# A decoder block on one core: the branch weights moved behind z's steps with a third place, one combine moved behind them, and half of z's first tokens reloaded as rows

## The chip, the cores and the metric

The kernel runs on one core of a Trainium2 chip. A core has five engines that work side by side, each on its own queue of instructions: TensorE (PE, matrix products; its weight loads are listed apart as PEld), VectorE (DVE), ScalarE (ACT), GpSimd (POOL) and SyncE (SP, which here only issues transfers). Transfers are carried by sixteen DMA engines and may be issued by SP, POOL and ACT. An engine starts an instruction only when the instruction ahead of it on its own queue is under way and the semaphores that it names are up, so an instruction that waits also holds all that stands behind it on that engine. The metric is the device time of one launch in microseconds (us).

## The reference

The reference is one layer of a decoder on 2,048 tokens of width 1,024, all in 32-bit floats. Cut to what matters:

```python
h = rmsnorm(x, norm_pre_mix)
proj = h @ w_in                       # q k v | u z | gate_a gate_b
y_attn = dilated_attention(rope(q), rope(k), v)          # three groups, softmax over the groups
z = layernorm(gelu(proj_z))                              # 512 channels
sz = w_spatial (lower triangle, per 128 tokens) @ z + b_spatial
y_gmlp = gelu(proj_u) * sz
merged = sigmoid(gate_a) * (y_attn @ w_branch_attn) + sigmoid(gate_b) * (y_gmlp @ w_branch_gmlp)
x = x + rmsnorm(merged @ w_out, norm_post_mix)
x = x + rmsnorm(relu(rmsnorm(x) @ w_mlp_in) ** 2 @ w_mlp_out, norm_post_mlp)
```

`y_attn` combines three groups of heads: per token and head the three partial outputs are scaled by a softmax over three log-denominators and added. The kernel calls that step the combine.

## The kernel before

The tokens are worked in four chunks of 512 (0 to 3), and chunks in two halves (0 and 1 are half 0). Every 32-bit operand of a large product is kept as two parts, a high part (`hi`, the value rounded to the matmul's type) and a low part (`lo`, value minus `hi`), and `mm3` (L94) makes one product of three matmuls: hi·hi, hi·lo and lo·hi (L95, L96, L97). `split` (L67) makes the two parts from a raw value: a copy that rounds (L70 on ACT, L72 on POOL) and a subtraction (L78, on DVE or POOL).

Most of the program is written as generators that PE steps through: `steps(n)` advances the matmul stream (`fill`) by n steps of three matmuls, and the code between two calls places work of the other engines there. On PE the order of the instructions is the written one. On the other engines a scheduler may move an instruction, but what stands in `with behind():` is issued only after the instruction of each of these engines that stands ahead of it in the program.

The stretch that this document is about is the end of the input products, before the branches are merged:

- `gates()` (L666) makes the gate and u columns. In its last phase (half 0) it also issues from a list `ins`, one entry a step (two at two of the steps), the loads of the next stage: `hT_b0`, the normalised tokens of chunk 0 transposed (both parts, eight loads of 512 KB from `hb_d`, where the parts were stored), and `w_z0`, the z weights (eight loads of 512 KB from `wz_d`). Raw tokens lie in `hT_d` too. An entry of the list `todo` is split between, by ACT and POOL. The tiles `ga0` to `ga11` hold gate and u columns on their way out.
- z of half 0: `z_00` to `z_03` (chunk 0) and `z_10` to `z_13` (chunk 1), each eight steps over the eight blocks k of the width. Steps are counted by `n` in the loop at L1091. On the way it loads `hT_b1` (raw rows, four loads) and splits them (ACT and POOL, at n 12, 15, 18, 21), loads and splits the six branch weights `wb0` to `wb5` (`load_wb`, `split_wb`: POOL issues the load and rounds, DVE subtracts), and works the last chunk's combine. A branch weight's raw rows `wbraw` (512 KB) lie in one of two places; a load into a place waits for the DVE subtraction of the weight that lay there.
- the combine of chunk 1 (L964) reads its partial outputs from `cw`. DVE makes maximum `M`, differences `E`, then ACT the exponential, DVE the sums `Z`, the reciprocal and the scaled `E`; ACT and DVE scale the outputs (L990, L993), DVE adds them (L995, L996), PE transposes the result (`yt_10`, `yt_11`, L1001), ACT copies it and stores it to `yad`.
- the merge of chunk 2 begins behind z: `load_y` brings six operands `yt`, all split by POOL (twelve operations); `b` are the products with the branch weights, `gates` the gate columns, multiplied in by DVE (L1189); `sz` is the spatial product of `z`; `woraw` are raw rows of the output weights.

Two waits on SP belong to the picture. Eight semaphores are used in turn for the transfers that SP and ACT issue, and a transfer waits until the earlier one on its semaphore has landed. So `early_gates` (L1144) waits for the two stores `yad` of the last combine.

Of the kernel before, what the change touches and what calls it, by code (L numbers as in the profile page):

```python
# [8 lines left out]
F32 = mybir.dt.float32  # L9
# [7 lines left out]
P = 128  # L17
S = 2048
D = 1024
# [8 lines left out]
def f32(ap):  # L28
    return ap.bitcast(F32) if ap.dtype != F32 else ap
# [12 lines left out]
def block_kernel(ctx, tc, a, out):  # L42
    nc = tc.nc
    pe, act, dve, pool, sp = nc.tensor, nc.scalar, nc.vector, nc.gpsimd, nc.sync
    x = a["x"]

    def stack(es, name, bufs=1, side=None, space=None):
        kw = dict(name=name, bufs=bufs, reuse_waits="tile")
        if side:
            kw["side"] = side  # L50
        if space is not None:
            kw["space"] = space
        return es.enter_context(tc.tile_pool(**kw))
# [13 lines left out]
    def split(hi, lo, src, hi_eng="act", lo_eng="dve"):  # L67

        if hi_eng == "act":
            act.activation(hi, src, AF.Copy)  # L70
        elif hi_eng == "pool":
            pool.tensor_scalar(hi, src, 1.0, 1.0, op0=OP.mult, op1=OP.mult)  # L72
        else:
            dve.tensor_copy(hi, src)
        if behind_product is not None and lo_eng == "dve":
            behind_product.append((lo, src, f32(hi)))
        else:
            (pool if lo_eng == "pool" else dve).tensor_sub(lo, src, f32(hi))  # L78
# [70 lines left out]
    hT_d = dtile([4, P, KT, 512], "hTd")  # L149
# [15 lines left out]
    e1 = ExitStack()  # L165
    hp = stack(e1, "hp", 1)
    wp = stack(e1, "wp", 2)
# [7 lines left out]
    def behind():  # L175

        es, t = ExitStack(), mybir.EngineType
        for e in (t.Activation, t.DVE, t.Pool, t.SP):
            es.enter_context(tc.issue_after(next(i for i in reversed(nc.cur_bb.bb.instructions) if i.engine == e)))
        return es  # L180

    hT = {}
# [178 lines left out]
    with ExitStack() as e1a:  # L361
# [118 lines left out]
        for half in range(2):  # L480
# [19 lines left out]
            for n, (g, which) in enumerate(qk):  # L500
                w = nxt
# [112 lines left out]
    LAST = len(seq) - PAIRS[0]  # L614
# [51 lines left out]
    def gates():  # L666

        bank, todo, out_, ins = {}, [], [], []
        slots = [None, hp.tile([P, 2, 2, 4, 512], F32R, name="opB", tag="hT", bufs=2)]
        zs = wp.tile([P, 8, 512], F32, name="gz", tag="w", bufs=3)  # L670
        zs = [zs[:, n] for n in range(8)]
        xs = [st.tile([P, 512], F32, name=f"gx{n}", tag="ev", bufs=3) for n in range(3)]
        g_["b"].update({(1, 1): hT[2][:, :, :4], (1, 2): hT[2][:, :, 4:]})
        phases = [(half, ops) for half in (1, 0) for ops in PHASES]
        starts, t = {}, 0
        for n, (half, ops) in enumerate(phases):
            starts[t] = n
            t += PAIRS[half] * len(ops)
        for t, (half, i, n) in enumerate(seq):
            if t in starts:  # L680
                ph, t0 = starts[t], t
                if ph + 1 < len(phases):
                    s = (ph + 1) % 2
                    if not slots[s]:
                        slots[s] = hp.tile([P, 2, 2, 4, 512], F32R, name="opA", tag="hT", bufs=2)
                    for j, i2 in enumerate(phases[ph + 1][1]):
                        new = operand(phases[ph + 1][0], i2, slots[s][:, j])
                        ins += new[0]
                        todo += new[1]
                else:  # L690
                    hs = reload_h(0)
                    ins += hs[:4] + ws[4:6] + hs[4:6] + ws[6:] + hs[6:]
            elif todo and (t - t0) % 3 == 1 and t > t0 + 1:
                w, k = todo.pop(0)
                with behind():
                    split(w[:, 0, k:k + 2], w[:, 1, k:k + 2], f32(w)[:, 1, k:k + 2], "act", "pool")
            if t == LAST - 4:
                ws = want(5)
                ins += ws[:4]
            if t == LAST:  # L700
                g_["ends"] = g_["vs"] + zs[8:]
            for n_ in (t + PIECES,) if t < LAST else {0: (4, 5), 1: (6, 7), 2: (8,), 3: (9,)}.get(t - LAST, ()):
                piece(n_ if t < LAST else LAST + n_)
            split_piece(t + SPLITS)
            if i in (1, 6, 5, 4):
                bank[n] = psum_mm(f"g{half}{i}{n}")
            p, w, h = bank[n], g_["w"].pop(t), g_["b"][half, i]
            for k in range(4):
                for m, (l, r) in enumerate(((0, 0), (0, 1), (1, 0))):
                    pe.matmul(p, w[:, l, k], h[:, r, k], start=i in (1, 6, 5, 4) and not k and not m,  # L710
                              stop=k == 3 and m == 2, skip_group_check=True)
                if (t, k) == (3, 2) and late:
                    sz_out(*late.pop(0))
                yield
            if t == 3:
                a = [ga.tile([P, 512], F32, name=f"ga{n_}", tag=f"ga{n_}", bufs=1) for n_ in range(12)]
                xs += a[:7]
                zs += a[7:9]
                vs = a[9:11]
                g_["vs"] = vs + xs[8:] + zs[8:]  # L720
                g_["raws"] += a[11:]
            x, z, fn = xs[n], zs[n], AF.Copy if n < 8 else AF.Gelu_apprx_tanh
            while out_:
                sp.dma_start(*out_.pop())
            for _ in range(2 if half and i == 4 or t in (LAST + 5, LAST + 7) else 1):
                if ins:
                    sp.dma_start(*ins.pop(0))
            if i == 1:
                act.activation(x, p, AF.Copy)
            elif i == 2:  # L730
                act.activation(z, p, fn)
                o = z, 0, 0
            elif i == 6:
                dve.tensor_add(z, x, p)
            elif i == 7:
                dve.tensor_add(x, x, p)
            elif i == 5:
                if (half, n) == (0, 0):
                    g_["vs"] = a[9:11]
                v = g_["vs"].pop(0)  # L740
                g_["vs"].append(v)
                dve.tensor_add(v, x, p)  # L742
                o = v, 1, 1
            elif i == 3:
                dve.tensor_add(z, z, p)
                o = z, 0, 1
            else:
                dve.tensor_add(x, x, p)  # L748
                o = x, 1, 0
            if n > 7 and i in (5, 3, 4):  # L750
                act.activation(o[0], o[0], fn)
            if i in (2, 5, 3, 4):
                c, dst = 2 * half + o[2], gate_d if n < 8 else u_d
                out_.append((dst[n % 8 * 2 + o[1], :, c * 512:(c + 1) * 512], o[0]))
        sp.dma_start(*out_.pop())
        yield
# [302 lines left out]
    def combined(*order):  # L1059
        for n, k in order:  # L1060
            steps(n)
            with behind():
                next(cs[k])

    combined((0, 0), (4, 1), (8, 0), (3, 0), (3, 0), (2, 2), (6, 1), (3, 1), (3, 1), (1, 0),
             (10, 2), (3, 2), (3, 2), (1, 1), (19, 2))
    steps(75 - 69)
    ec.close()
    ega.close()

    e2r = ExitStack()
    wbp = stack(e2r, "wbp", 1, side="right")
    wb = [wbp.tile([P, 2, D], F32R, name=f"wb{k}") for k in range(6)]
    wb_raw = {}

    def load_wb(k):
        wb_raw[k] = wp.tile([P, D], F32, name=f"wbraw{k}", tag="raw", bufs=2)
        pool.dma_start(wb_raw[k], a["w_branch"][:, k, :])

    def split_wb(k):  # L1080
        with behind():
            split(wb[k][:, 0], wb[k][:, 1], wb_raw.pop(k), "pool", "dve")
# [4 lines left out]
    next(sg)  # L1087
    while not cw:
        steps(1)
    todo = {22: (3,), 24: (3,), 27: (3,), 38: (3,)}  # L1090
    for n in range(1, 56):  # L1091
        steps(1)
        if zin:
            sp.dma_start(*zin.pop(0))
        if n in (12, 15, 18, 21):
            k, h = (n - 12) // 3 * 2, hT[1]
            with behind():
                split(h[:, 0, k:k + 2], h[:, 1, k:k + 2], f32(h)[:, 1, k:k + 2], "act", "pool")
        if n in (24, 28, 32, 36, 42, 48):
            split_wb((24, 28, 32, 36, 42, 48).index(n))  # L1100
        if n in (4, 6, 25, 29, 33, 37):
            load_wb((4, 6, 25, 29, 33, 37).index(n))
        if n == 48:
            next(sg)
        for k in todo.get(n, ()):
            combined((0, k))
# [402 lines left out]
    for n, c in enumerate(chunks):  # L1509
        if n:  # L1510
            mg = merge(c, yt, {0: flush, 2: flush}, merge_sums if c == 0 else merge_sums_last if c == 1 else None)
        for i in range(4):
# [10 lines left out]
            if n == 3 and i == 1:  # L1523
# [7 lines left out]
                for o, (q, n_) in enumerate(FIRST):  # L1531
                    raw = gtp.tile([P, 512], F32, name=f"ar{n_}_{q}", tag=f"gt{o % 2}", bufs=3 - o % 2)
# [234 lines left out]
    for n, z in enumerate(last_ones):  # L1767
# [28 lines left out]
        elif n == 9:  # L1796
# [4 lines left out]
            w = s1p.tile([P, 2, 512], F32R, name="spot0")  # L1801
# [33 lines left out]
    begun, ybank, left, todo = set(), {}, {}, {}  # L1835
# [128 lines left out]
    for k, (_, n, i) in enumerate(yorder):  # L1964
# [10 lines left out]
        if i == 1 and more:  # L1975
# [6 lines left out]
            if nth in (4, 5) and g + 1 < NQ // 2 - 1:  # L1982
                w = 2 * g + nth - 2
# [102 lines left out]
```

## Time and profile before

| what | time |
|---|---|
| three runs | 2663.45, 2666.44 and 2670.65 us, median 2666.44 |
| the profiled execution | 2663.08 us, span 2661.4 us |
| PE busy | 2619.8 us, 98% of the span |
| z of half 0, from its first matmul to the first of the merge's `b` | 1015.66 to 1077.2 us of the span |

Times in the rows below are microseconds from the start of the span. A row of the timeline has start, duration, engine, line, operation, the tile written and the tiles read, and how many alike are put together (x4); in square brackets stands how long the engine had been idle before it and what ended that. A row of waits has engine, line, operation that waited and what it waited for, then the sum of the waits, their count and the longest. In a row of the windows stand, after the stretch's length, the busy time and the number of instructions of PE, PEld, DVE, ACT and POOL, then the clock that was granted to TensorE (1 is full speed), the share of the DMA engines' time that was busy, and GB/s.

### The profile page before, as it was taken

What the parts mean: (1) busy time and instruction counts of PE and PEld (TensorE: products, weight loads), DVE (VectorE), ACT (ScalarE), POOL (GpSimd) and SP (SyncE); (2) the same over time, 40 slices, a digit from 0 to 9 for tenths busy, and PEclk for the clock granted to TensorE, in tenths of its full rate; (3) what the DMA queues carried; (4) which work ended last, traced back from release to release, by engine and by line L of the source; (5) the groups of instructions that cost most, each with busy time, mean ns of one, the idle gap of its engine ahead of it and who ended that gap; (6) DMA issues with size and microseconds to landing.
All of it is one profiled execution on the core that took longest, in us unless ns stands there. A gap on an engine that the chain in (4) does not pass through costs nothing. (4 is left out here: it accounts for less than half of the span.)

```text
span 2661.4 us, 35503 instructions
## 1 busy us (share of the span) xinstructions
PE 2619.8 (98%) x12458; PEld 2186.9 (82%) x12458; DVE 1665.8 (63%) x2793; ACT 1090.9 (41%) x2283; POOL 1207.1 (45%) x1099
## 2 busy tenths in 40 slices
PE   9999999999999998999999999999999999999998
PEld 8888888888888886788878888888888888888886
DVE  5676665535443466755676665645437888888866
ACT  5213111254455443444446555655545333323334
POOL 0363354374454554311324463233215776676645
PEclk9999999999999998999999999999999999999999
DMA  8779778888888897744556464644343222222235
GB/s 319 285 246 323 266 228 289 294 282 248 291 287 242 236 310 277 242 154 153 207 199 254 146 225 149 222 139 119 119 147 107 87 71 73 87 88 87 87 115 210
DMA packets 389285, 526.21 MB, mean 198 GB/s; under 512 B 57009, under 2 KB 242097, under 8 KB 388082
## 3 DMA queue, kind: packets, MB, share of 16 engines
q1 hardware_dynamic: 299472, 430.79, 49.5%
q0 software_dynamic: 15856, 54.80, 5.5%
q10 hardware_dynamic: 73778, 38.35, 4.8%
q8 instruction: 98, 1.61, 0.3%
q14 instruction: 81, 0.66, 0.1%
HBM read 340.67 MB, written 183.17 MB: 197 GB/s over the span
## 5 line engine op out<-in xcount | busy, mean ns | idle before, releaser
L1937 PE MATMUL ya<-T_spots,s 128*128 128x512 f32 x1176 | 289.3, 390 | 0.7 <-ACT T_spots L70 0.6
L70 ACT ACTIVATE s<-sraw 128x768 fp32r<-128x768 f32 (+1 forms) x184 | 127.2, 696 | 330.3 <-POOL sraw L1738 155.7
L1937 PEld LDWEIGHTS ya<-T_spots,s 128*128 128x128 f32 x1176 | 220.6, 188 | 47.3 <-ACT T_spots L70 0.9
L78 DVE TENSOR_TENSOR s<-sraw,s 128x512 fp32r<-128x512 f32 x172 | 184.1, 1095 | 8.5 <-ACT s L70 8.5
L1408 PE MATMUL aa<-B,A 128*128 128x512 f32 x768 | 182.4, 390 | 1.5 <-ACT xs L1422 0.9
L1379 POOL TENSOR_TENSOR s<-w1r 128x512 f32<-128x512 f32 x32 | 42.3, 1322 | 308.7 <-DVE S L78 256.1
L710 PE MATMUL g<-opA,spots 128*128 128x512 f32 x672 | 171.4, 399 | 1.9 <-DVE cv L742 1.9
L1408 PEld LDWEIGHTS aa<-B,A 128*128 128x128 f32 x768 | 143.9, 188 | 32.0 <-ACT xs L1422 1.3
L710 PE MATMUL g<-opB,spots 128*128 128x512 f32 x648 | 164.3, 398 | 0.2 <-DVE ga L748 0.2
L1937 PE MATMUL yc<-T_spots,s 128*128 128x512 f32 x624 | 159.7, 389 | 0.0
L95 PE MATMUL x<-hT_a,wq 128*128 128x512 f32 x384 | 149.8, 390 | 0.0
L97 PE MATMUL x<-hT_a,wq 128*128 128x512 f32 x384 | 149.6, 389 | 0.0
L96 PE MATMUL x<-hT_a,wq 128*128 128x512 f32 x384 | 149.6, 389 | 0.0
L710 PEld LDWEIGHTS g<-opA,spots 128*128 128x128 f32 x672 | 121.6, 189 | 23.9 <-issue 2.2
L78 POOL TENSOR_TENSOR spots<-gr,spots 128x512 fp32r<-128x512 f32 x98 | 127.5, 1304 | 22.7 <-DMA gr<-in_w_in_dram 15.7
L1937 PEld LDWEIGHTS yc<-T_spots,s 128*128 128x128 f32 x624 | 117.2, 188 | 24.3
L710 PEld LDWEIGHTS g<-opB,spots 128*128 128x128 f32 x648 | 116.9, 189 | 21.6 <-issue 0.6
L70 ACT ACTIVATE hl<-r 128x512 fp32r<-128x512 f32 x48 | 30.4, 632 | 235.4 <-POOL r L321 89.0
L960 DVE TENSOR_REDUCE o<-po 128x256 f32<-128x512 f32 x48 | 33.2, 692 | 133.6 <-PE po L959 133.5
L1737 POOL TENSOR_TENSOR sraw<-sraw 128x256 f32<-128x256 f32 x56 | 41.8, 747 | 161.8 <-DVE s L78 158.8
L72 POOL TENSOR_SCALAR spots<-gr 128x512 fp32r<-128x512 f32 x86 | 54.9, 638 | 132.1 <-PE g L710 100.7
L78 POOL TENSOR_TENSOR T_spots<-w2r,T_spots 128x512 fp32r<-128x512 f32 x70 | 104.4, 1519 | 7.3 <-ACT T_spots L70 7.3
(427 smaller groups left out, 6990.3 us busy)
## 6 DMA issues: line engine op xcount, KB each, us to landing
w1r<-in_w_mlp_in_dram SPq DMA_DIRECT2D x64, 512.0 KB, 3.8
sraw<-sd SPq DMA_DIRECT2D x128, 256.0 KB, 3.2
qk<-hl SPq DMA_DIRECT2D x24, 1024.0 KB, 5.7
qq<-qk SPq DMA_DIRECT2D x96, 256.0 KB, 5.2
w2r<-in_w_mlp_out_dram SPq DMA_DIRECT2D x16, 1024.0 KB, 7.8
sd<-u ACTq DMA_DIRECT2D x63, 256.0 KB, 3.5
g<-gated SPq DMA_DIRECT2D x58, 256.0 KB, 4.7
gr<-sgd SPq DMA_DIRECT2D x53, 256.0 KB, 4.8
```

Of the source, the lines that this page charges most:

```text
L70: act.activation(hi, src, AF.Copy)
L72: pool.tensor_scalar(hi, src, 1.0, 1.0, op0=OP.mult, op1=OP.mult)
L78: (pool if lo_eng == "pool" else dve).tensor_sub(lo, src, f32(hi))
L95: pe.matmul(ps, lh, rh, start=start, stop=False)
L96: pe.matmul(ps, lh, rl, start=False, stop=False)
L97: pe.matmul(ps, ll, rh, start=False, stop=stop)
L710: pe.matmul(p, w[:, l, k], h[:, r, k], start=i in (1, 6, 5, 4) and not k and not m, stop=k == 3 and m == 2, skip_group_check=True)
L960: dve.tensor_reduce(ot[:, :, j * 64:(j + 1) * 64], po.rearrange("p (b h e) -> p b e h", b=4, h=2), axis=AX.X, op=OP.add)
L1379: pool.tensor_add(s1, a21, a22)
L1408: pe.matmul(p, w[:, l, k, :], h[:, r, k, :], start=i in (1, 6, 5) and not k and not n, stop=k == 3 and n == 2, skip_group_check=True)
L1737: pool.tensor_add(a22, a21, a22)
L1937: pe.matmul(p, s[:, l], w[r], start=i in (1, 2, 5) and not m and not o, stop=m == 1 and o == 2, skip_group_check=True)
```

## The change

Four things are changed, all between about 970 and 1090 us of the span.

- In `gates()`, of the eight loads of `hT_b0` the first four (both parts of k 0 to 3) are replaced by two loads of raw rows from `hT_d` into the place of the low part. ACT and DVE split them (ACT rounds, DVE subtracts). The list `ins` has ten entries where it had twelve, and 1 MB less is read.
- A third place for branch weights, `wr`, laid over `ga0` and `ga1`, takes `wbraw2` and `wbraw5`. The loads now stand behind what is ahead of them, at n 8, 9, 10, 23, 25, 27 (before 4, 6, 25, 29, 33, 37), and the splits at n 23, 25, 27, 36, 38, 40 (before 24, 28, 32, 36, 42, 48).
- The combine of chunk 1 moves from n 22, 24, 27, 38 to n 43, 45, 48, 60, behind all splits of branch weights; the loop is six steps longer.
- The order of the other chunks' combines within the attention's tail is changed by one or two steps.

```diff
                     hs = reload_h(0)
-                    ins += hs[:4] + ws[4:6] + hs[4:6] + ws[6:] + hs[6:]
+                    h0 = f32(hT[0])
+                    rows = [(h0[:, 1, k:k + 2], hT_d[0][:, k:k + 2]) for k in (0, 2)]
+                    ins += rows + ws[4:6] + hs[4:6] + ws[6:] + hs[6:]
+                    todo += [(hT[0], 0), (hT[0], 2)]
             elif todo and (t - t0) % 3 == 1 and t > t0 + 1:
                 w, k = todo.pop(0)
                 with behind():
-                    split(w[:, 0, k:k + 2], w[:, 1, k:k + 2], f32(w)[:, 1, k:k + 2], "act", "pool")
+                    split(w[:, 0, k:k + 2], w[:, 1, k:k + 2], f32(w)[:, 1, k:k + 2], "act",
+                          "pool" if t < LAST else "dve")
...
-    combined((0, 0), (4, 1), (8, 0), (3, 0), (3, 0), (2, 2), (6, 1), (3, 1), (3, 1), (1, 0),
-             (10, 2), (3, 2), (3, 2), (1, 1), (19, 2))
+    combined((0, 0), (4, 1), (6, 0), (3, 0), (4, 0), (1, 2), (8, 1), (3, 1), (3, 0), (2, 1),
+             (8, 2), (4, 2), (3, 2), (1, 1), (19, 2))
...
+    wr = stack(e1, "wr", 1)
...
     def load_wb(k):
-        wb_raw[k] = wp.tile([P, D], F32, name=f"wbraw{k}", tag="raw", bufs=2)
-        pool.dma_start(wb_raw[k], a["w_branch"][:, k, :])
+        wb_raw[k] = wr.tile([P, D], F32, name=f"wbraw{k}", tag="wr", bufs=1) if k % 3 == 2 else \
+            wp.tile([P, D], F32, name=f"wbraw{k}", tag="raw", bufs=2)
+        with behind():
+            pool.dma_start(wb_raw[k], a["w_branch"][:, k, :])
...
-    todo = {22: (3,), 24: (3,), 27: (3,), 38: (3,)}
-    for n in range(1, 56):
+    todo = {43: (3,), 45: (3,), 48: (3,), 60: (3,)}
+    for n in range(1, 62):
...
-        if n in (24, 28, 32, 36, 42, 48):
-            split_wb((24, 28, 32, 36, 42, 48).index(n))
-        if n in (4, 6, 25, 29, 33, 37):
-            load_wb((4, 6, 25, 29, 33, 37).index(n))
+        if n in (23, 25, 27, 36, 38, 40):
+            split_wb((23, 25, 27, 36, 38, 40).index(n))
+        if n in (8, 9, 10, 23, 25, 27):
+            load_wb((8, 9, 10, 23, 25, 27).index(n))
```

How the instructions stand on three queues, before and with the change:

PE, at the transposes of the combine of chunk 1 (`cw` holds its result, `ident` the unit matrix, `z_1x` is z's group x of 128 tokens in chunk 1). Before:

```order
L95 MATMUL z_10_9819<-w_z0_1_9198,hT_b1_9622 128x512 [waits Activation_49]
L96 MATMUL z_10_9819<-w_z0_1_9198,hT_b1_9622 128x512
L97 MATMUL z_10_9819<-w_z0_1_9198,hT_b1_9622 128x512 [waits Pool_49]
L1001 MATMUL yt_10_9849<-ident_93,cw_9618 128x128 [waits DMAHW1_49,DVE_49,PE_49]
L1001 MATMUL yt_10_9849<-ident_93,cw_9618 128x128 [waits Activation_49] x3
L1001 MATMUL yt_11_9857<-ident_93,cw_9618 128x128 [waits PE_49]
L1001 MATMUL yt_11_9857<-ident_93,cw_9618 128x128 x2
L1001 MATMUL yt_11_9857<-ident_93,cw_9618 128x128 [waits Activation_49]
L95 MATMUL z_10_9819<-w_z0_1_9198,hT_b1_9622 128x512
```

With the change:

```order
L97 MATMUL z_13_9929<-w_z0_1_9202,hT_b1_9627 128x512
L1005 MATMUL yt_10_9945<-ident_93,cw_9623 128x128 [waits DMAHW7_49,DVE_49,PE_49]
L1005 MATMUL yt_10_9945<-ident_93,cw_9623 128x128 [waits Activation_49] x3
L1005 MATMUL yt_11_9953<-ident_93,cw_9623 128x128 [waits PE_49]
L1005 MATMUL yt_11_9953<-ident_93,cw_9623 128x128 x2
L1005 MATMUL yt_11_9953<-ident_93,cw_9623 128x128 [waits Activation_49]
L95 MATMUL z_13_9929<-w_z0_1_9202,hT_b1_9627 128x512
```

The transposes stood ahead of the last step of `z_10`; they now stand behind the fifth step of `z_13`, 22 steps (66 matmuls) later.

DVE, at the combine of chunk 1 and the subtractions of the branch weights. Before:

```order
L976 TENSOR_TENSOR E_1_9724<-cw_9618,M_1_9721 128x4x4 x2
L577 BN_STATS bs_02_9743<-z_0_9623 128x6 [waits Activation_49]
L578 BN_AGGR mv_0_9624<-bs_02_9743 128x2 [waits DVE_49]
L980 TENSOR_TENSOR Z_1_9729<-E_1_9724,cw_9618 128x4x4 [waits Activation_49]
L980 TENSOR_TENSOR Z_1_9729<-E_1_9724,cw_9618 128x4x4 x2
L981 TENSOR_TENSOR M_1_9721<-Z_1_9729 128x16 [waits DVE_49]
L78 TENSOR_TENSOR wb0_9594<-wbraw0_9645,wb0_9594 128x1024 [waits DMAHW4_49,DMAHW3_49,DMAHW5_49,DMASW0_49,Pool_49]
```

With the change:

```order
L582 TENSOR_SCALAR z_0_9628<-z_0_9628,mv_0_9629,r_ln0_9776 128x512 x3
L78 TENSOR_TENSOR wb2_9601<-wbraw2_9677,wb2_9601 128x1024 [waits DMASW2_49,Pool_49]
L577 BN_STATS bs_10_9822<-z_1_9790 128x6 [waits Activation_49]
L578 BN_AGGR mv_1_9791<-bs_10_9822 128x2 [waits DVE_49]
L78 TENSOR_TENSOR wb3_9602<-wbraw3_9733,wb3_9602 128x1024 [waits DMASW3_49,Pool_49]
L78 TENSOR_TENSOR wb4_9603<-wbraw4_9748,wb4_9603 128x1024 [waits DMASW4_49,Pool_49]
L78 TENSOR_TENSOR wb5_9604<-wbraw5_9758,wb5_9604 128x1024 [waits DMAHW2_49,DMAHW1_49,DMAHW3_49,DMAHW0_49,DMAHW5_49,DMASW5_49,Pool_49]
L976 TENSOR_TENSOR M_1_9840<-cw_9623 128x16 [waits DMAHW7_49,DMAHW0_49]
```

The combine's first operation stood ahead of the first subtraction of a branch weight; it now stands behind the sixth, which waits for the load of `wbraw5`.

SP, at the last loads of z's operands (`gated` and `ud` are stores of gate and u columns). Before:

```order
L727 DMA w_z0_1_9198<-wzd_85 128x1024 [waits DMAHW1_49]
L727 DMA w_z0_1_9198<-wzd_85 128x1024 [waits DMAHW3_49]
L724 DMA gated_73<-ga4_4530 128x512 [waits DMAHW4_49,DVE_49]
L727 DMA hT_b0_9333<-hbd_84 128x1024 [waits DMAHW5_49]
L724 DMA ud_72<-ga5_4531 128x512 [waits DMAHW6_49,Activation_49]
L727 DMA hT_b0_9333<-hbd_84 128x1024 [waits DMAHW7_49]
```

With the change:

```order
L731 DMA w_z0_1_9202<-wzd_85 128x1024 [waits DMAHW6_49]
L728 DMA gated_73<-ga3_4529 128x512 [waits DMAHW7_49,DVE_49]
L731 DMA hT_b0_9333<-hbd_84 128x1024 [waits DMAHW1_49]
L731 DMA hT_b0_9333<-hbd_84 128x1024 [waits DMAHW3_49]
L728 DMA gated_73<-ga4_4530 128x512 [waits DMAHW4_49,DVE_49]
L728 DMA ud_72<-ga5_4531 128x512 [waits DMAHW5_49,Activation_49]
```

The last two loads of `hT_b0` stood behind the stores of `ga4` and `ga5`; they now stand, side by side, ahead of both, where the last two loads of `w_z0` stood.

## The prediction

> **What bounds the kernel now.** I read the page first, then PE's waits, PE's timeline at those waits, the windows around them, and last the queues of the engines that end them. The page says that PE has no room:
>
> ```profile
> span 2661.4 us, 35503 instructions
> PE 2619.8 (98%) x12458; PEld 2186.9 (82%) x12458; DVE 1665.8 (63%) x2793; ACT 1090.9 (41%) x2283; POOL 1207.1 (45%) x1099
> ```
>
> The change takes no matmul away, so it can only move waits. These are PE's between 1005 and 1135 us:
>
> ```profile
> PE yt L1001 <- issue: 6.3, 1, 6.3
> PE z L95 <- DMA hT_b<-hbd: 4.2, 1, 4.2
> PE b L96 <- POOL yt L78: 1.9, 3, 1.3
> PE o L95 <- ACT mg L70: 1.4, 1, 1.4
> PE b L95 <- DVE g L1189: 1.0, 1, 1.0
> PE z L97 <- DMA hT_b<-hbd: 1.0, 2, 0.6
> ```
>
> Three are in reach: z waits 5.2 us for its first tokens, the transposes of the combine 6.3, and the merge's `b` 1.9 for POOL. Each is dearer than its idle time, as the timeline shows:
>
> ```profile
> 1024.77 0.77 PE L95 MATMUL z<-w_z,hT_b 128*128 128x512 f32 x1 [4.20 <-DMA hT_b<-hbd]
> ...
> 1044.83 0.39 PE L95 MATMUL z<-w_z,hT_b 128*128 128x512 f32 x1
> 1045.06 0.39 PE L96 MATMUL z<-w_z,hT_b 128*128 128x512 f32 x1
> ...
> 1056.73 1.94 PE L1001 MATMUL yt<-ident,cw 128*128 128x128 f32 x8 [6.30 <-issue]
> ...
> 1084.70 5.30 PE L554 MATMUL sz<-wsp,z 128*128 128x128 f32 x32
> ```
>
> Matmuls start 0.23 us apart in the middle rows (23 of them from 1044.83 to 1050.04 give 0.227), but behind a wait at about half the speed: ten in the five microseconds of the first row here, whose seventh column, the granted clock, says why:
>
> ```profile
> 1025.00:1030.00 5.00, 4.36 (x10) 2.98 (x11) 0.66 (x1) 0.60 (x1) 0.00 (x0) 0.51 1.06 385
> 1084.20:1087.60 3.40, 3.40 (x16) 3.25 (x17) 3.40 (x7) 0.11 (x1) 0.00 (x0) 0.55 1.02 350
> ```
>
> **z's first tokens: a gain of 3.6.** SP issues the last operands in these rows (the DMA share, the column behind the clock, is 1.06 and 1.02 above, so bytes count):
>
> ```profile
> 1012.56 2.96 SPq L727 DMA_DIRECT2D w_z<-wzd  x2
> 1017.10 0.32 SPq L727 DMA_DIRECT2D hT_b<-hbd  x1
> 1020.28 0.32 SPq L727 DMA_DIRECT2D hT_b<-hbd  x1
> ...
> w_z<-wzd SPq DMA_DIRECT2D x1, 512.0 KB, 8.9
> ...
> w_z<-wzd SPq DMA_DIRECT2D x1, 512.0 KB, 7.6
> ```
>
> The first row groups the issues at 1012.56 and 1015.21; the last two are their times to landing, so these land at 1021.5 and 1022.8. With two list entries fewer, the last two `hT_b` loads stand in those two places. PE wants the first at 1020.57 (1024.77 less 4.20) and the second two matmuls on: about 0.9 and 0.9 us of waiting remain, beside the 0.4 at 1019 that stays. Idle falls from 5.2 to 2.2, a gain of 3.0. Of the half clock (4.8 us from 1024.77, worth 2.4) I keep one window of 3.4 us, worth 1.7: another 0.7. If no slow window comes it is 5.3; if the third early branch weight (512 KB, now issued at about 1012) comes first in the queues, 1.3 (512 KB at some 400 GB/s) is lost: 2.3. The splits of the rows (two copies on ACT and two subtractions on DVE, each of 1,024 columns and so some 1.2 by the row of L996 further on) fall in a stretch where both engines have room:
>
> ```profile
> 1010.00:1015.00 5.00, 5.00 (x28) 4.21 (x27) 1.54 (x3) 2.21 (x3) 0.00 (x0) 1.00 0.90 248
> ```
>
> They cost nothing while the rows land by about 1010; the first landed at 996 in the place they take. The shifts of the other chunks' combines by one or two steps are at nothing too: PE has no wait there, before or, by the order, after.
>
> **The combine: a loss of 8.4.** In the new order PE comes to `yt_10` 66 matmuls later: 1050.43 (1056.73 less 6.30), plus 66 times 0.227, less 3.6: 1061.8. What it needs is now behind all six branch weights on DVE, so I follow that queue.
>
> ```profile
> 1036.45 4.75 POOL L78 TENSOR_TENSOR hT_b<-hT_b 128x1024 fp32r<-128x1024 f32 x2 [4.45 <-ACT hT_b L70]
> 1041.89 4.75 POOL L78 TENSOR_TENSOR hT_b<-hT_b 128x1024 fp32r<-128x1024 f32 x2 [0.69 <-ACT hT_b L70]
> ...
> 1058.18 0.58 POOL L1078 DMA_DIRECT2D wbraw<-in_w_branch_dram  x1 [7.25 <-DVE t_ln L110]
> 1058.79 1.06 POOL L72 TENSOR_SCALAR wb<-wbraw 128x1024 fp32r<-128x1024 f32 x1
> ...
> 1071.90 0.63 POOL L72 TENSOR_SCALAR yt<-yt 128x512 fp32r<-128x512 f32 x1
> 1072.61 2.13 POOL L78 TENSOR_TENSOR yt<-yt 128x512 fp32r<-128x512 f32 x1
> ...
> 1081.50 2.51 POOL L78 TENSOR_TENSOR yt<-yt 128x512 fp32r<-128x512 f32 x2
> ```
>
> POOL's work on `hT_b1` ends at 1046.6; with z 3.6 earlier, at 1043.0. Then come the first weight's rounding (1.06) and subtraction (1.22), to 1045.3; the second, behind a load issue of 0.58 and its own rounding and subtraction, to 1048.2; z's first normalisation on DVE (1.9 for its four large operations, 1.4 for small ones), to 1051.5; the third subtraction, to 1052.7. Only then is the place for `wbraw5` free. A branch weight takes 5.0 to land, the median in the view of `wbraw`:
>
> ```profile
> DMA to landing us min/median/max: 4.3/5.0/7.1
> ```
>
> So `wbraw5` is there at 1057.7, rounded at 1058.8, subtracted at about 1060.4; the third place spares the fourth and fifth weight, not the sixth. From there the combine runs. In the trace its operations run like this (the last row is ACT's, of the scaling):
>
> ```profile
> 1036.48 2.40 DVE L973 TENSOR_TENSOR M<-M,cw 128x16 f32<-128x16 f32 x1
> ...
> 1044.35 3.35 DVE L980 TENSOR_TENSOR Z<-E,cw 128x16 f32<-128x16 f32 x3 [2.12 <-ACT E L977]
> ...
> 1055.40 1.23 DVE L996 TENSOR_TENSOR cw<-cw 128x1024 f32<-128x1024 f32 x1
> ...
> 1049.64 3.93 ACT L990 ACTIVATE cw<-cw,E 128x64 f32<-128x64 f32 x16 [3.33 <-DVE E L985]
> ```
>
> One comparison of 16 columns took 2.40, ending with POOL's subtraction of `hT_b` beside it: a small DVE operation waits for the POOL operation under way. In the new order POOL's twelve `yt` operations (1071.90 to 1084.01, 12.1) follow the sixth rounding at 1058.8 at once and last to about 1071: they lie exactly beside the combine. What that costs each is in the same twelve's present neighbours:
>
> ```profile
> 1079.23 1.16 DVE L104 TENSOR_SCALAR v_ln<-mv 128x4 f32<-128x4 f32 x1
> ...
> 1084.07 1.91 DVE L582 TENSOR_SCALAR z<-z,mv,r_ln 128x512 f32<-128x512 f32 x4
> 1085.89 1.28 DVE L1189 TENSOR_TENSOR gates<-gates,b 128x512 f32<-128x512 f32 x2
> ...
> 1094.52 1.27 DVE L1189 TENSOR_TENSOR gates<-gates,b 128x512 f32<-128x512 f32 x2
> ```
>
> From the first of these rows to the third, six small operations take 4.8, some 0.9 each with their gaps. So, from 1060.4: five (`M`, `E`) 4.6 to 1065.0; the exponential 2.1 to 1067.1; three `Z` 2.8 to 1069.9; then, with POOL nearly done, six small ones 1.6 to 1071.5; sixteen scalings on ACT 3.9 to 1075.4 (DVE's two scalings and first addition, some 1.2 each, fit beside them); the last addition 1.2 to 1076.7. PE goes on there, after 14.9 us instead of 6.3. If nothing contended, the fourteen small operations would take 3.3, and it would be 1070.5: 8.7. If all fourteen contended, at the 1.1 that each of the three `Z` takes in the row above (3.35), it would be about 1083: 21. I take 14.7, next to the middle one, since its rows are those of the same twelve POOL operations. The slow clock behind it (about 2) is there before and after. Term: 8.4.
>
> The Trainium skill ("SBUF — State Buffer", on the two sides of SBUF and who interferes with whom) states that DVE and GpSimd share a port pair as an exclusive lock, and that a DVE instruction with two SBUF inputs contends for it. The 2.40 agrees; by the rule the wait is the 14.9 above, and without it the sum below would come out about 6 to 8 lower.
>
> **The merge's start: a gain of 3.4.** POOL's `yt` work is done at 1071 and `b` begins at 1077.2 plus 4.8 (8.4 less 3.6): 1082. The three waits (1.9) go, and so does the slow window of 1084.2, in which 32 `sz` matmuls took 5.30; at the usual rate they take about 3.7. POOL, DVE and the weights are all ahead of PE there. If the window behind `yt_10`'s stall falls on `b` instead, 1.5 of it stays.
>
> **The gates: a loss of 2.3.** This is who waits next. SP's queue holds the first two gate columns until the combine's two stores have landed:
>
> ```profile
> SPq L1152 <- DMA yad<-ya: 15.5, 2, 15.3
> ...
> 1063.76 0.85 SPq L1152 DMA_DIRECT2D gates<-gated  x2
> ```
>
> Their issue follows `yt_10` by 7.0 (1063.76 less 1056.73). With `yt_10` at 1076.7 it is 1083.7, the columns land 5.0 later, the sigmoid some 0.7 (like other operations on 512 columns here), and DVE's first product with a gate stands at 1089.4 instead of 1085.89: 3.5 late, where PE by the three terms so far is 1.4 late. DVE, the third number pair, is nearly full from there:
>
> ```profile
> 1090.00:1110.00 20.00, 20.00 (x105) 17.12 (x105) 18.29 (x24) 7.03 (x12) 6.43 (x7) 1.00 0.75 234
> ```
>
> PE waits for it at 1119.15 (the row of 1.0) and for ACT behind it (1.4), so the end goes with DVE: at most 2.3 more, taken whole. The raw output weights and the other gate columns queue behind on SP and come some 6 us later too; I cost that at nothing, since DVE takes the second pair of gates only at 1094.52, 8.6 behind the first. At the low end of the combine's range this term is nothing.
>
> **The sum** is 8.4 less 3.6 less 3.4 plus 2.3: 3.7. On the profiled execution (2663.08, that is 3.4 below the median of the three runs) this gives 2666.8, on the median 2670.1. I forecast 2670. About 0.3%, 8 us, is what a measurement here can tell from no change, so this counts as the same.
>
> **The rivals.**
> - The combine runs unhindered. For it: three `Z` took 3.35 beside one long subtraction, so two of them passed freely. Against it: the 2.40, and the 4.8. PE waits 8.7, the gates are in time: 2.4 (8.7 less 6.3) less 3.6 less 3.4, minus 4.6: 2661.8. If z's slow window goes as well (1.7) and the sixth weight lands 2 earlier, it crosses 8 below.
> - The slower side: POOL's `yt` work stretches over the whole combine. Alone such a subtraction takes 1.26 (two in 2.51 at 1081.50), beside DVE's work 2.13 (1072.61). If all six take 2.1, POOL ends past 1076 and covers all fourteen small operations; `yt_10` comes at 1083 instead of 1076.9, and these 6 pass through gates and DVE: plus 9.7, 2676.1. It decides from where POOL's last `yt` operation ends after about 1073.
> - The change doesn't do what it says at z: the third branch weight's 512 KB and the deeper queue delay the last two loads, and only 1 us is gained: plus 6.3, 2672.7. For it: the two took 7.5 and 6.3 to land; against it: the `w_z` rows, which landed from the same places.
>
> **How the numbers follow.** The forecast gets 0.50, the unhindered combine 0.17, the stretched POOL 0.25, the lost gain at z 0.08. The first rival crosses minus 8 in half of its cases, the second plus 8 in most, the third rarely, the forecast in few: faster 0.08, same 0.66, slower 0.26. The range goes from the first rival's sum, 2661, to some 3 above the second's, 2678.
>
> **What would show it.** z's first group should end near 1025, not 1028.5. `yt` should wait 12 to 17 with DVE's last addition at its end, `M` start near 1060 behind the sixth subtraction, and POOL's `yt` splits lie beside `M` to `Z`. `b` should not wait for POOL, and the first gate loads be issued after 1082. A wait at `yt` under 9, or above 19, or one for `hT_b` that is still 4, makes the prediction wrong in the place named.

## The result, and the profile after

| | before | with the change |
|---|---|---|
| median of twelve runs | 2666.24 us | 2669.35 us |
| lowest and highest | 2660.51 to 2670.73 | 2664.24 to 2673.31 |
| ratio, 95% interval | | 1.001, 1.0 to 1.002 |
| profiled execution: span | 2661.4 us | 2668.5 us |

The change costs about 3 us, one part in a thousand; the interval runs from 0 to 5. The two profiled executions differ by 7.1, of which 4.1 lie before z begins (1019.78 for 1015.66). They arise far ahead of all that is changed: the first gate product starts at 521.0 for 516.5, and in the kernels below it starts at 515.9 to 523.1. Starts are therefore compared from z's first matmul. PE's waits between 1005 and 1140 us, with the change:

```profile
PE yt L1005 <- issue: 14.1, 1, 14.1
PE z L95 <- DMA hT_b<-hbd: 3.0, 1, 3.0
PE b L95 <- DVE g L1196: 2.9, 2, 2.2
PE o L95 <- ACT mg L70: 0.9, 1, 0.9
PE z L97 <- DMA hT_b<-hbd: 0.2, 1, 0.2
```

The wait at the combine's transposes has gone from 6.3 to 14.1; z's is down from 5.2 to 3.2; `b` no longer waits for POOL and waits longer for DVE. The views of the tiles `z`, `b` and `o` give the first and last start of their matmuls in the window (the two numbers joined by "to"):

```profile
L95 PE MATMUL z<-w_z,hT_b x64: 387/389/799, 1019.8 to 1087.3; 128*128 128x512 f32 x64
L95 PE MATMUL b<-yt,wb x48: 389/389/735, 1088.2 to 1132.9; 128*128 128x512 f32 x48
L95 PE MATMUL o<-wo,mg x136: 389/389/499, 1133.6 to 1299.4; 128*128 128x512 f32 x136
```

From z's start to the first `b` it is 68.5 us (61.8 before: 1077.46 less 1015.66; the 1077.2 given above is the start of the last z matmul), to the first `o` 113.8 (108.1 before: 1123.74). So this stretch is 5.7 longer. From there to the end the changed kernel's execution took 2.8 less (1534.9 for 1537.7), in code that is the same; the other kernels below took 1532.9 to 1539.9 there, so I read that as scatter.

The windows show where the clock is slow (the seventh number, counts in brackets left out): in two windows behind z's wait, and behind the transposes.

```profile
1027.00:1030.50 3.50, 3.27 (x7) 2.19 (x8) 0.00 (x0) 0.00 (x0) 0.00 (x0) 0.50 1.05 382
1030.50:1034.00 3.50, 3.50 (x12) 2.73 (x11) 0.88 (x2) 0.60 (x1) 0.00 (x0) 0.61 0.97 321
1069.00:1083.00 14.00, 0.02 (x1) 0.05 (x1) 13.67 (x25) 6.05 (x19) 10.12 (x10) 0.56 0.00 1
1083.00:1088.20 5.20, 5.20 (x17) 4.48 (x18) 0.00 (x0) 1.20 (x2) 0.00 (x0) 0.53 0.30 111
```

The third row is the stall itself: PE does nothing, the DMA engines do nothing, DVE is busy for 13.67 of 14 us. DVE's timeline in it, from the sixth weight's subtraction to the last addition:

```profile
1066.14 1.63 DVE L78 TENSOR_TENSOR wb<-wbraw,wb 128x1024 fp32r<-128x1024 f32 x1 [0.94 <-POOL wb L72]
1067.70 1.26 DVE L976 TENSOR_TENSOR M<-cw 128x16 f32<-128x16 f32 x1
...
1069.82 1.66 DVE L980 TENSOR_TENSOR E<-cw,M 128x16 f32<-128x16 f32 x3
...
1072.24 2.29 DVE L984 TENSOR_TENSOR Z<-E,cw 128x16 f32<-128x16 f32 x3
...
1075.44 1.51 DVE L989 TENSOR_TENSOR E<-E,M 128x16 f32<-128x16 f32 x3
...
1081.65 1.23 DVE L1000 TENSOR_TENSOR cw<-cw 128x1024 f32<-128x1024 f32 x1
```

And POOL's, beside it:

```profile
1066.08 0.61 POOL L72 TENSOR_SCALAR yt<-yt 128x512 fp32r<-128x512 f32 x1
1066.78 2.14 POOL L78 TENSOR_TENSOR yt<-yt 128x512 fp32r<-128x512 f32 x1
...
1072.00 2.50 POOL L78 TENSOR_TENSOR yt<-yt 128x512 fp32r<-128x512 f32 x2
...
1075.65 3.56 POOL L78 TENSOR_TENSOR yt<-yt 128x512 fp32r<-128x512 f32 x2
```

The combine starts behind the sixth weight, runs beside POOL's twelve operations (1066.08 to 1079.21), and takes 15.2 us from its first maximum to the end of its last addition (1067.70 to 1082.88). The first maximum, of 16 columns, ends at 1068.96, as POOL's first subtraction does (1068.92); the three `Z` end at 1074.53, as its third and fourth do (1074.50). PE goes on at 1082.98, 0.1 behind the last addition; "issue" in the row of its wait says only that the profile names no releaser.

### The profile page after: what moved, and what is told of

Read it like the earlier page. It is cut to its first block, busy times and chain, and to the rows that moved or that the text cites. A ratio compares the mean times of both kernels' runs of the same rounds, so it can differ in the third digit from the quotient of the medians.

```text
span 2668.5 us, 35509 instructions
## 1 busy us (share of the span) xinstructions
PE 2619.9 (98%) x12458; PEld 2186.6 (82%) x12458; DVE 1659.5 (62%) x2795; ACT 1094.2 (41%) x2285; POOL 1212.2 (45%) x1099
```

## The experiments

Times are medians with the ratio to the kernel before, of the runs made beside them, and its 95% interval. The kernel before had medians of 2666.24, 2666.03, 2665.04 and 2663.74 us beside the change and the later groups of runs, so across rows the ratios compare better than the times. "z's wait" is the sum of PE's waits for `hT_b`, in one profile of each kernel; two profiles of `yt` off POOL gave 2.9 and 3.8.

| kernel | us | ratio, interval | z's wait | wait at yt_10 |
|---|---|---|---|---|
| before | 2666.2 | | 5.2 | 6.3 |
| the change | 2669.35 | 1.001 (1.0 to 1.002) | 3.2 | 14.1 |
| rows only | 2659.5 | 0.998 (0.9971 to 0.9989) | 1.4 | 8.0 |
| combine back | 2667.24 | 1.0005 (0.9996 to 1.0014) | 3.6 | 13.5 |
| transposes late | 2660.64 | 0.9975 (0.9963 to 0.9988) | 3.5 | none |
| yt off POOL | 2661.06 | 0.9985 (0.9977 to 0.9994) | 3.8 | 8.4 |
| third load later | 2668.48 | 1.0015 (1.0005 to 1.0024) | 3.3 | 16.2 |
| old order of the other combines | 2667.41 | 1.0017 (1.0007 to 1.0027) | 1.2 | 17.1 |
| rows, transposes late | 2662.36 | 0.9993 (0.9981 to 1.0004) | 1.3 | 0.7 |
| combine first | 2656.98 | 0.9974 (0.9961 to 0.9987) | 2.1 | 0.7 |
| combine first, yt shared | 2656.05 | 0.9969 (0.9959 to 0.9979) | 2.4 | 2.4 |
| the same, old order | 2654.50 | 0.9964 (0.9951 to 0.9977) | 1.8 | 0.9 |

The theory to begin with was the prediction's: the combine behind six branch weights, slowed by POOL, costs more than z's earlier start gives. The rivals were that the weights' loads and splits at their new steps lose the time wherever the combine stands, and that POOL has no part in it.

### Is it POOL's work beside the combine?

The changed kernel with the six `yt` operands split by ACT and DVE:

```diff
-    yt = load_y(2, ("pool", "pool"))
+    yt = load_y(2)
```

> The changed kernel with the six yt operands of the merge split by ACT and DVE, not POOL, so that POOL is idle beside the combine. Theory (half of the wait at yt_10 is DVE's small operations waiting for POOL's yt operations): the wait at yt_10 falls from 14 to 8 or 9, the combine from its first maximum to its last addition from 15.2 to 10 or 11; the splits then come behind the combine on ACT and DVE and b waits for them, so the whole time says little. Rival (the wait is the queue of branch weights and the chain itself): the wait stays at 12 to 14, and the chain at 14 or more.

Measured: 8.4 at `yt_10`. The row of PE's wait, then DVE's timeline:

```profile
PE yt L1005 <- issue: 8.4, 1, 8.4
```

```profile
1065.58 0.17 DVE L976 TENSOR_TENSOR M<-cw 128x16 f32<-128x16 f32 x1
...
1066.61 0.33 DVE L980 TENSOR_TENSOR E<-cw,M 128x16 f32<-128x16 f32 x3
...
1067.70 0.33 DVE L984 TENSOR_TENSOR Z<-E,cw 128x16 f32<-128x16 f32 x3
...
1073.30 1.23 DVE L1000 TENSOR_TENSOR cw<-cw 128x1024 f32<-128x1024 f32 x1
```

The same operations take 0.17 for 1.26, 0.33 for 1.66, 0.33 for 2.29, and the combine 8.9 us (1065.58 to 1074.53) for 15.2. POOL's share of the wait is 5.7, as the theory had it; the combine is shorter than the 10 or 11 expected. The same kernel was then timed:

> The changed kernel with the yt operands split by ACT and DVE, timed (one look gave a wait of 8.4 at yt_10 and one time of 2660.9). Theory (the wait for POOL's yt operations costs the changed kernel 5.7 at yt_10, of which b's wait for ACT and DVE gives back 2 to 4, and DVE's merge starts as late): 2662 to 2666, 3 to 7 under the changed kernel. Rival (one time told too much): 2667 to 2670.

It is 2661.06, ratio 0.9985: 8 us under the changed kernel by the medians, some 7 by the ratios, at the upper end of the theory's 3 to 7 or just past it. In this run's profile PE again waits 8.4 at `yt_10`, and `b` waits 2.9 for ACT's copies and little for DVE. Taking POOL's splits away thus turns the change from slightly slower to slightly faster; the two intervals do not meet.

### What do the parts give alone?

The kernel before with the rows alone:

```diff
-                    ins += hs[:4] + ws[4:6] + hs[4:6] + ws[6:] + hs[6:]
+                    h0 = f32(hT[0])
+                    rows = [(h0[:, 1, k:k + 2], hT_d[0][:, k:k + 2]) for k in (0, 2)]
+                    ins += rows + ws[4:6] + hs[4:6] + ws[6:] + hs[6:]
+                    todo += [(hT[0], 0), (hT[0], 2)]
```

> The kernel before with the rows alone (first four loads of hT_b0 replaced by two loads of raw rows, split by ACT and DVE). Theory (z's part of the change is worth what its own waits and slow clock lose): in the changed kernel z waited 3.2 us where it waited 5.2, and the slow clock lasted longer, so 1 to 2 us are gained at z; the combine's chain hangs on loads that come as much earlier, so the gain stays: 2663 to 2666. Rival A (as the prediction put it): the wait falls to about 2.2 and 3.6 us are gained: 2661 to 2664. Rival B: the combine's chain does not come earlier, the wait at yt_10 grows by what z gains, and the time is that of before.

It gained more than each of the three had it: 2659.5, ratio 0.998, 2.9 to 7.7 under the kernel before. z waits 1.4, and the wait at `yt_10` grows by only 1.7:

```profile
PE yt L1005 <- issue: 8.0, 1, 8.0
PE b L95 <- DVE g L1193: 2.2, 1, 2.2
PE b L96 <- POOL yt L78: 1.9, 3, 1.3
PE z L97 <- DMA hT_b<-hbd: 1.0, 1, 1.0
PE z L95 <- DMA hT_b<-hbd: 0.4, 1, 0.4
```

The changed kernel holds the same rows, and z waits 3.2 there. The next question is for the rest. The changed kernel with the combine at its old steps:

```diff
-    todo = {43: (3,), 45: (3,), 48: (3,), 60: (3,)}
+    todo = {22: (3,), 24: (3,), 27: (3,), 38: (3,)}
```

> The changed kernel with the combine of chunk 1 back at n 22, 24, 27 and 38; rows, third place and earlier branch weights stay. Theory (the combine behind the six branch weights is what the change loses): PE waits about 6 at yt_10 as before, POOL is done with its yt splits before the merge's b, so these waits go, and the gates are in time: 6 to 9 us faster than the changed kernel, 2659 to 2664. Rival (the loads and splits of the branch weights at their new steps lose the time, wherever the combine stands): within 3 of the changed kernel.

The theory's times fell here: 2667.24, no better than the kernel before and not told apart from the changed one, and PE still waits 13.5 at `yt_10`. The row of the wait, then DVE's timeline, say what for:

```profile
PE yt L1005 <- DVE cw L1000: 13.5, 1, 13.5
```

```profile
1049.56 1.22 DVE L997 TENSOR_TENSOR cw<-cw,E 128x1024 f32<-128x1024 f32 x1
1050.70 0.69 DVE L577 BATCH_NORM_STATS2 bs<-z 128x6 f32<-128x512 f32 x1
1051.30 1.53 DVE L997 TENSOR_TENSOR cw<-cw,E 128x1024 f32<-128x1024 f32 x1
1052.75 1.21 DVE L78 TENSOR_TENSOR wb<-wbraw,wb 128x1024 fp32r<-128x1024 f32 x1
...
1056.47 1.23 DVE L78 TENSOR_TENSOR wb<-wbraw,wb 128x1024 fp32r<-128x1024 f32 x1
1057.62 1.22 DVE L999 TENSOR_TENSOR cw<-cw 128x1024 f32<-128x1024 f32 x1
1058.75 1.27 DVE L582 TENSOR_SCALAR z<-z,mv,r_ln 128x512 f32<-128x512 f32 x1
1059.94 2.04 DVE L1000 TENSOR_TENSOR cw<-cw 128x1024 f32<-128x1024 f32 x1
```

Between the combine's second scaling and its first addition now stand two weights' subtractions and the small operations of z's normalisation: 4.8 us. The last addition ends 45.8 behind z's start, where it ended 41.0 behind it before, and PE comes to the transposes 2.2 earlier: together all but 0.2 of the 7.2 by which the wait has grown. By this trace the rival was half right: the weights' splits at their new steps cost time, because they stand inside the combine's chain on DVE. Two kernels follow that up. First the transposes alone stay late:

```diff
-    todo = {43: (3,), 45: (3,), 48: (3,), 60: (3,)}
+    todo = {22: (3,), 24: (3,), 27: (3,), 60: (3,)}
```

> The changed kernel with the combine's work on DVE and ACT back at n 22, 24 and 27, and only its transposes on PE at n 60. Theory: DVE's last addition is done some 5 us before PE comes there, so no wait at yt_10; PE then comes to the merge's b some 13 us earlier than in the changed kernel and waits there for POOL's yt splits, about 5 us, until the sixth weight's rounding plus 12: 8 to 12 us faster than the kernel before the change, 2654 to 2659. Rival (PE's waits there only move: b waits for POOL as long as yt_10 waited for DVE): within 3 us of the kernel with the whole combine back.

2660.64, ratio 0.9975: under the kernel before by 3 to 10, if 2 above what was expected, and 7 under the kernel with the whole combine back, so the rival is out. PE does not wait at `yt_10`; `b` waits 3.3 for POOL. From the changed kernel this one differs only in the place of the combine's work on DVE and ACT: so that place, behind the six branch weights, is what costs the change its wait of 14.1 and, by the ratios, some 9 us. Second, the combine's additions are placed ahead of the second weight's split, the transposes where the sum is done:

```diff
-    todo = {43: (3,), 45: (3,), 48: (3,), 60: (3,)}
+    todo = {22: (3,), 23: (3,), 24: (3,), 47: (3,)}
...
-        if n in (8, 9, 10, 23, 25, 27):
-            load_wb((8, 9, 10, 23, 25, 27).index(n))
+        if n in (8, 9, 14, 23, 25, 27):
+            load_wb((8, 9, 14, 23, 25, 27).index(n))
```

> The kernel of the run before with the combine's DVE and ACT work at n 22, 23, 24, ahead of the second weight's split, and its transposes at n 47. Theory (with the combine back at its old steps PE waited 13.5 us because the second and third weight's subtractions and a normalisation stood between its scalings and its additions): DVE's last addition is done about 38 us behind z's start instead of 46, PE does not wait at yt_10 or under 2, the merge's b waits for POOL's yt splits as with the late transposes, 3 to 5: 2656 to 2660, 6 to 10 under the kernel before the change. Rival (DVE and ACT bound the merge, so an earlier b gives nothing): no better than the rows alone, 2660 to 2663.

2656.98, ratio 0.9974, in the expected range. Its waits:

```profile
PE b L96 <- POOL yt L78: 4.9, 4, 1.7
PE b L95 <- DVE g L1196: 2.6, 1, 2.6
PE z L95 <- DMA hT_b<-hbd: 1.4, 1, 1.4
PE yt L1005 <- PE z L97: 0.7, 1, 0.7
```

The last addition ends at 1053.14, 37.7 behind z's start (1015.47), 8.1 earlier than with the combine back: the order on DVE does what the trace said. In time this kernel and the one with late transposes are not told apart (0.9974 and 0.9975). The largest wait is now for POOL's `yt` work (4.9). Without the earlier weights that is dearer still, as the rows alone with late transposes show:

```diff
-    todo = {22: (3,), 24: (3,), 27: (3,), 38: (3,)}
+    todo = {22: (3,), 24: (3,), 27: (3,), 49: (3,)}
```

> The kernel with the rows alone, and the combine's transposes at n 49, not 38; loads and splits of the branch weights stay as before the change, in two places. Theory (without the earlier weights the merge's b waits for POOL's yt splits what yt_10 no longer waits for DVE, so the third place is what lets the rest pay): no wait at yt_10, b waits 8 to 10 for POOL, the time is that of the rows alone, 2658 to 2661. Rival (the transposes' place alone was the fault): 3 us or more faster than the rows alone, under 2656.

```profile
PE b L95 <- POOL yt L72: 5.4, 1, 5.4
PE b L96 <- POOL yt L78: 3.7, 4, 1.4
```

As the theory had it, `b` waits 9.1 for POOL and the kernel is no faster than the rows alone (2662.36, 1 above the expected range). The wait had only moved. That the third place and the earlier weights pay, once the combine is not behind them, is likely but not shown: the intervals of the two kernels above meet those of the rows alone and of this one.

### Who delays z's last two loads?

Two guesses. The first, the early load of `wbraw2`:

> The changed kernel with one load moved: wbraw2 is loaded at n 14, behind POOL's first subtraction of hT_b1, not at n 10, ahead of z. Theory (these 512 KB share the DMA engines with the last two loads of hT_b0, and that is why z waited 3.2 us in the changed kernel and 1.4 with the rows alone): z waits 1.0 to 1.8, and the time is 1 to 3 us under the changed kernel, 2666 to 2668. Rival (the order of the other chunks' combines, whose stores now lie beside these loads, is what delays them): z still waits about 3.

This changes `load_wb`'s steps as shown above and nothing else. z waited 3.3, as its rival said, and the time was that of the changed kernel: the theory fell. The second, the order of the other chunks' combines, set back in that same kernel:

```diff
-    combined((0, 0), (4, 1), (6, 0), (3, 0), (4, 0), (1, 2), (8, 1), (3, 1), (3, 0), (2, 1),
-             (8, 2), (4, 2), (3, 2), (1, 1), (19, 2))
+    combined((0, 0), (4, 1), (8, 0), (3, 0), (3, 0), (2, 2), (6, 1), (3, 1), (3, 1), (1, 0),
+             (10, 2), (3, 2), (3, 2), (1, 1), (19, 2))
```

> The changed kernel with wbraw2 loaded at n 14 and the order of the other chunks' combines as it was before the change. Theory (with wbraw2 moved z still waited 3.3, so the new order's stores lie beside the last two loads of hT_b0 and delay them): z waits 1.0 to 1.8 as with the rows alone, and the time is 1 to 3 us under the changed kernel, 2666 to 2668. Rival (one profile of each: the waits of 1.4 and of 3.3 are the same thing at different luck): 2.5 to 3.5.

```profile
PE yt L1005 <- issue: 17.1, 1, 17.1
...
PE z L95 <- DMA hT_b<-hbd: 0.7, 1, 0.7
PE z L97 <- DMA hT_b<-hbd: 0.5, 1, 0.5
```

z waits 1.2. In the table the four kernels with the rows and the old order wait 1.2 to 1.8, those with the rows and the new one 2.1 to 3.8; so the order has a part, though which transfer it is was not tried. But the time does not follow: 2667.41, still above the kernel before. PE came to `yt_10` 4.8 us earlier (44.3 behind z's start for 49.1) and waited 3 longer, since the combine hangs on the weights. Most of what z gains is lost there.

### A faster kernel

POOL's `yt` work shared with DVE, in the kernel with the combine first:

```diff
-    yt = load_y(2, ("pool", "pool"))
+    yt = load_y(2, ("pool", "dve"))
```

> The same with the low parts of the six yt operands on DVE, POOL rounding only. Theory (POOL's yt subtractions hold the merge's b and DVE's small operations): b waits under 2, DVE's first product with a gate comes 1 to 3 us earlier than with POOL doing both: 2654 to 2658. Rival (DVE is the fuller engine there, and its 4 us more come back in the merge): 1 to 3 us slower than with POOL doing both.

2656.05: inside the expected range, but 1 us from the kernel it is compared with, which the intervals do not tell apart. The wait had moved again: `b` waits 3.4 for DVE's subtractions, where under 2 for all was expected. With the old order of the other combines as well:

> The fastest kernel so far (combine first, transposes at n 47, yt shared between POOL and DVE) with the old order of the other chunks' combines. Theory as for the run above: z's wait falls from 2.4 to under 1.8, 1 us faster: 2653 to 2657. Rival: the new order is worth something elsewhere, 1 to 4 slower: 2657 to 2661.

2654.5, ratio 0.9964 (0.9951 to 0.9977): 6 to 13 us under the kernel before, and the lowest of all, though its interval meets those of the two before it. z waits 1.8; `b` still waits 3.9 for DVE's `yt` subtractions.

## Why the prediction was right, and where not

The forecast was 2670, measured 2669.35; the difference to before was put at 3.7 and is 3.1. The terms, in the profiled executions:

| term | forecast | measured |
|---|---|---|
| z's first tokens | -3.6 | -1.5 |
| the wait at yt_10 and the clock behind it | +8.4 | +7.8 and +0.4 |
| the merge's start | -3.4 | -4.7 |
| the gates | +2.3 | +3.7 |
| from z's start to `o` | +3.7 | +5.7 |
| ahead of z | 0 | +4.1, scatter |
| behind the start of `o` | 0 | -2.8, scatter |

The measured values are differences of starts from z's: PE comes to `yt_10` at 49.1, where the old pace would be 50.6 (34.8, 66 matmuls of 0.227, and the 0.9 that `rowsum`, two products of the spatial weights that now stand ahead, and the slow matmul behind it take); first `b` 6.7 later; the second group of `b` (1095.85 and 1089.75) 2.0 later; `o` 5.7 later.

That the median came within 1 us of the forecast is in part luck. In the traces the four terms add up to 5.7, not 3.7; two of them missed by some 2 and 1.4 on the slow side, one by 1.3 on the fast side. Small slips in the prediction's own sums (3.0 and 0.7 taken as 3.6, a wait of 14.9 taken as 14.7, 3.5 less 1.4 taken as 2.3) are of 0.1 to 0.2 each.

**The combine** went as worked out: a wait of 14.1 for 14.9, the chain beside POOL 15.2 for 16.3, and without POOL the wait is 8.4 for 8.7. Its parts fit less well and cancel: the first five small operations took 3.8 for 4.6, the exponential 0.8 for 2.1, the six behind `Z` 2.5 for 1.6, and the end 6.0 for 5.2, since DVE's own four large operations set it, not ACT's scalings. The Trainium skill's rule of the exclusive lock ("SBUF — State Buffer", who interferes with whom) agrees with both waits, 14.1 beside POOL's work and 8.4 without it.

**z's first tokens** gained less. Counted from z's start, the two loads were issued where the prediction put them or earlier, but they (issued at 1016.63 and 1019.1) took 10.4 and 9.3 us to land, where 8.9 and 7.6 were counted:

```profile
1016.63 2.81 SPq L731 DMA_DIRECT2D hT_b<-hbd  x2
...
hT_b<-hbd SPq DMA_DIRECT2D x1, 512.0 KB, 10.4
...
hT_b<-hbd SPq DMA_DIRECT2D x1, 512.0 KB, 9.3
```

So they were there 7.3 and 8.6 behind z's start instead of 5.8 and 7.2. The step that failed is "The shifts of the other chunks' combines by one or two steps are at nothing too": with the old order the wait is 1.2, no slow clock follows it, and PE gains 6.3 at z. How the new order delays the loads stays open. The slow pace then lasted 5.8 us (1027.06 to 1032.88), where one window of 3.4 was taken. The rival cause, the third weight's load, did not hold.

**The merge's start**: no wait for POOL, as forecast, and 32 `sz` at full clock in 3.5 us. It is 1.3 more than taken because the 18 matmuls of `b` ahead of `sz` took 7.2 us before (1077.46 to 1084.70), where 18 of 0.227 take 4.1: they lost 3.1, and the row of the waits that the prediction used shows 1.9 of it.

**The gates**: DVE's first product with a gate came at 1093.53, 3.5 later than before from z's start, as forecast to the tenth, but not for the reason given; the agreement is luck. These are ACT's and DVE's timelines:

```profile
1088.45 0.60 ACT L575 ACTIVATE z<-z 128x512 f32<-128x512 f32 x1 [2.75 <-PE z L97]
...
1091.97 1.15 ACT L1179 ACTIVATE gates<-gates 128x512 f32<-128x512 f32 x2
```

```profile
1089.08 0.69 DVE L577 BATCH_NORM_STATS2 bs<-z 128x6 f32<-128x512 f32 x1 [6.20 <-ACT z L575]
...
1091.70 1.92 DVE L582 TENSOR_SCALAR z<-z,mv,r_ln 128x512 f32<-128x512 f32 x4
1093.53 1.27 DVE L1196 TENSOR_TENSOR gates<-gates,b 128x512 f32<-128x512 f32 x2
```

The first gate column had landed at 1089.5 and both, by the sigmoid's row, ahead of 1092. DVE was busy until 1093.5 with the normalisation of the last z group, which the late transposes had pushed back with the rest of z; the sigmoids were done 0.4 earlier. The steps that failed are "Their issue follows `yt_10` by 7.0" (it was 4.0: 1087.01 less 1082.98), the 5.0 for landing (3.0 in the median), and that the product waits for the gates at all. That rests on the trace; no run tests it. The end did go with DVE: of the 3.7, 1.9 are longer waits for it (2.9 for 1.0), and most of the rest is a slow stretch behind the longer of them (a granted clock of 0.52 from 1128.7 to 1132.2).

**The rivals**: an unhindered combine needs POOL's work elsewhere, as the run with `yt` off POOL shows; a stretched POOL did not come (its last `yt` operation ended 3.7 us ahead of DVE's last addition, and the six small operations behind `Z` were only partly held). The third rival, that only 1 us is gained at z, came close to what z did (1.5), though by the combines' order and not by the third weight's load; its sum for the difference to before, 6.3, is nearer the 5.7 of the traces than the forecast's 3.7.

## What to carry to other kernels

Read the order of an engine's queue before moving a chain onto it: what matters is which operations of another chain now stand inside or ahead of it, and a chain put behind a load waits for the load to land whatever its own length (here 4.1 us for `wbraw5`). A small DVE operation beside a stretch of POOL work can wait for the rest of the POOL operation under way (the first maximum took 1.26 for 0.17); here it made the chain 6.3 us longer, with fourteen small operations in it. Count them, or move the POOL work. And a wait taken away upstream is worth little while a later wait hangs on something else: with the old order z gained 6.3 us on the kernel before and PE then waited 10.8 longer at the next stall, while with the rows alone, in the kernel before, 4.7 of 6.1 came through to the first `b`.

## What was not expected

The first two gate columns, of 256 KB each, landed sooner than the prediction took: issued from 1087.01, in a median of 3.0 us where the same loads took 5.0 before. The DMA share was 0.00 in the stall ahead and 0.57 from 1087.0 to 1090.5, for 0.83 from 1063.7 to 1069.0 before; that this is the reason was not tested. The last row here is their issue and landing:

```profile
1087.01 1.36 SPq L1159 DMA_DIRECT2D gates<-gated  x2
...
gates<-gated SPq DMA_DIRECT2D x2, 256.0 KB, 3.0
```

And behind a wait of 3.0 PE's pace stayed low for 5.8 us (0.50 and 0.61 in the windows above), longer than the 5.0 behind the wait of 4.2 in the kernel before (1024.77 to 1029.75); the prediction took 3.4.
